# Sixteen transfers in place of twenty-four: joined tile loads and stores in a rotary-embedding kernel

## The chip, the cores and the metric

The kernel runs on one core of one Trainium2 chip. The metric is the device time of one execution in microseconds; the other cores are idle. The profile covers a span that is a little shorter than this time; the difference, 1.8 to 2.2 us, plays a part at the end of this study. DVE is the vector engine, POOL is GpSimd, PE the matrix engine, ACT the scalar engine; SP issues the transfers. PSUM is the small on-chip memory in which the kernel keeps its tables and products.

## The reference, cut to what matters

```python
batch, seq, dim = (16, 512, 1024)           # float32
num_heads = 16                              # head_dim 64, half_dim 32
x = x.reshape(batch, seq, num_heads, head_dim)
x1, x2 = x[..., :half_dim], x[..., half_dim:]
rotated = concatenate([x1 * cos - x2 * sin, x1 * sin + x2 * cos], axis=-1)
```

The input and the output are 33.55 MB each. Nothing is reused between batches, so each byte is moved once in and once out.

## The kernel before

Two batches make a tile of 128 partitions by 8 rows of 1024 numbers, 4 MiB; there are eight tiles and five buffers. DVE makes the cosine products and most sums, POOL most sine products, PE and ACT a part of the sums. Every transfer is issued by SP into one queue, which sixteen DMA engines work off. In the trace a tile is moved as 128 pieces of 32 KB, eight on each engine. A transfer has landed when its semaphore reports all of it; a seam is an engine's passage from one transfer to the next.

```python
def load(t, lo=0, hi=KK):
    if tiles[t] is None:
        tiles[t] = xp.tile([P, F], FP32, name="xt")          # pool of BUFS = 5
    s = slice(lo * dim, hi * dim)
    nc.sync.dma_start(out=tiles[t][:, s], in_=x_v[t][:, s])

load(0, 0, FIRST[0]) ... sin, cos ... rest of tile 0
for t in range(1, BUFS):
    load(t)
for i, n in enumerate(EXTRA):                                # four tiny loads
    nc.sync.dma_start(out=spare[:n, i], in_=sin_v[:n, :16])

tab = pfix.tile([P, BANK], FP32)                             # one PSUM tile for both tables
cos_t = tab[:, : KK * half]
sin_t = tab[:, KK * half : 2 * KK * half]

def stores(t):
    lo = 0
    for hi in LAST_OUT if t == NT - 1 else (KK,):            # LAST_OUT = (4, 8)
        store(t, lo, hi)
        lo = hi
    if t + 1 == NT - BUFS:                                   # after tile 2
        for n in range(BUFS, NT):
            load(n)                                          # tiles 5, 6, 7
# ... cut: the rotation itself, which the change does not touch
```

The tiny loads compute nothing. The transfers take eight semaphores in turn, and a transfer must wait for the one that had its semaphore eight places earlier. The tiny loads shift the count so that these waits fall where they do no harm.

## Time and profile before

| what | value | how to read it |
|---|---|---|
| time | 162.44 us | median of 3 runs, 162.35 to 162.64 |
| span of the profile | 160.7 us | first to last instruction of the program |
| DVE busy | 136.3 us, 85% | pauses only at the start and after its last tile |
| POOL busy | 127.1 us, 79% | second; waits for DVE to free its buffers |
| DMA queue | 98.0% of 16 engines' span | full from the second slice to the end |
| bytes | 67.25 MB | 33.69 read, 33.55 written |

The share of an engine that is busy does not by itself say what sets the end. Here two rows of the page are near full, DVE's and the DMA's.

### The profile page before, as it was taken

What the parts mean: (1) busy time and instruction counts of PE and PEld (TensorE: products, weight loads), DVE (VectorE), ACT (ScalarE), POOL (GpSimd) and SP (SyncE); (2) the same over time, 40 slices, a digit from 0 to 9 for tenths busy, and PEclk for the clock granted to TensorE, in tenths of its full rate; (3) what the DMA queues carried; (4) which work ended last, traced back from release to release, by engine and by line L of the source; (5) the groups of instructions that cost most, each with busy time, mean ns of one, the idle gap of its engine ahead of it and who ended that gap; (6) DMA issues with size and microseconds to landing.
All of it is one profiled execution on the core that took longest, in us unless ns stands there. A gap on an engine that the chain in (4) does not pass through costs nothing.

```text
span 160.7 us, 443 instructions
## 1 busy us (share of the span) xinstructions
PE 60.8 (38%) x71; PEld 19.3 (12%) x71; DVE 136.3 (85%) x85; ACT 18.7 (12%) x25; POOL 127.1 (79%) x38
## 2 busy tenths in 40 slices
PE   3041925056503931192308350664048402932000
PEld 0011301021102210131003010210022001300000
DVE  1059969999999999999999999999999999998000
ACT  0001311003000301012100310031003010211000
POOL 1039999999999999988998899898998899840000
PEclk9999995557655685559555855576556855595555
DMA  5999999999999999999999999999999999999994
GB/s 177 410 408 473 392 514 400 392 473 440 392 449 449 408 400 498 408 392 498 418 392 465 440 400 465 440 400 408 457 432 408 465 424 408 473 416 416 428 412 204
DMA packets 2787, 67.25 MB, mean 419 GB/s; under 512 B 354, under 2 KB 482, under 8 KB 482
## 3 DMA queue, kind: packets, MB, share of 16 engines
q1 hardware_dynamic: 2786, 67.24, 98.0%
q14 instruction: 1, 0.01, 0.0%
HBM read 33.69 MB, written 33.55 MB: 418 GB/s over the span
## 4 chain that ended last, share of the span: by engine, by line
DVE 68%; issue 12%; POOL 6%; DMA 4%; PE 1%; SPq 0%; DVEq 0%
DVE xt L189 33%; DVE pd L141 31%; POOL b L165 6%; DMA b<-in_sin_dram 4%; DVE pe_ps L141 3%; PE tab L113 1%; PE tab L114 1%; DVE sns L116 0%; DVE xt L150 0%; DVE own_ps L141 0%; SPq L74 0%; DVE sns L117 0%; DVEq L189 0%
## 5 line engine op out<-in xcount | busy, mean ns | idle before, releaser
L165 POOL TENSOR_TENSOR b<-xt,sns 128x2048 f32<-128x2048 f32 (+1 forms) x32 | 126.4, 3978 | 14.7 <-DVE sns L117 9.3
L189 DVE TENSOR_TENSOR xt<-pd,b 128x2048 f32<-128x2048 f32 x24 | 54.9, 2286 | 2.4 <-POOL b L165 1.6
L141 DVE TENSOR_TENSOR pd<-xt,tab 128x2048 f32<-128x2048 f32 x24 | 55.0, 2291 | 0.2
L176 PE MATMUL own_ps<-xt,ident 128*128 128x512 f32 x32 | 30.2, 1100 | 54.4 <-DVE xt L150 48.7
L176 PE MATMUL pe_ps<-b,ident 128*128 128x512 f32 x32 | 28.8, 1001 | 24.0 <-DVE pe_ps L141 24.0
L176 PEld LDWEIGHTS own_ps<-xt,ident 128*128 128x128 f32 x32 | 9.4, 323 | 74.3 <-DVE xt L150 59.7
L209 ACT COPY xt<-own_ps 128x1024 f32<-128x1024 f32 x8 | 8.1, 1012 | 73.7 <-PE own_ps L176 73.7
L181 ACT COPY xt<-pe_ps 128x512 f32<-128x512 f32 x16 | 9.4, 585 | 38.2 <-PE pe_ps L176 38.2
L176 PEld LDWEIGHTS pe_ps<-b,ident 128*128 128x128 f32 x32 | 8.4, 290 | 42.8 <-DVE pe_ps L141 34.1
L141 DVE TENSOR_TENSOR pe_ps<-xt,tab 128x512 f32<-128x512 f32 x16 | 11.0, 685 | 0.0
L141 DVE TENSOR_TENSOR own_ps<-xt,tab 128x1024 f32<-128x1024 f32 x8 | 9.8, 1223 | 0.0
L150 DVE TENSOR_TENSOR xt<-xt,tab 128x1024 f32<-128x1024 f32 x8 | 9.7, 1213 | 0.0
L116 DVE TENSOR_SCALAR sns<-tab 128x256 f32<-128x256 f32 x1 | 0.4, 424 | 8.2 <-PE tab L114 8.2
L113 PE MATMUL tab<-b,spread 64*128 64x256 f32 x2 | 1.2, 697 | 5.0 <-DMA b<-in_sin_dram 5.0
L209 ACT ACT_TABLE_LOAD x1 | 1.3, 1283 | 15.4 <-DVE xt L150 15.4
L101 PE MATMUL own_ps<-zero 128*128 128x512 bf16 x2 | 1.0, 618 | 1.2 <-DVE zero L97 1.2
L113 PEld LDWEIGHTS tab<-b,spread 64*128 64x128 f32 x2 | 0.5, 310 | 5.9 <-issue 5.9
L114 PE MATMUL tab<-b,spread 64*128 64x256 f32 x2 | 1.1, 631 | 0.0
L97 DVE MEMSET zero<- 128x256 uint32 x1 | 0.3, 272 | 0.9 <-PEq L240 0.9
L114 PEld LDWEIGHTS tab<-b,spread 64*128 64x128 f32 x2 | 0.7, 334 | 0.2
L101 PE MATMUL pe_ps<-zero 128*128 128x512 bf16 x1 | 0.6, 631 | 0.0
L101 PEld LDWEIGHTS <-zero 128*128 128x128 bf16 x3 | 0.3, 123 | 1.5 <-DVE zero L97 1.2
(9 smaller groups left out, 1.8 us busy)
## 6 DMA issues: line engine op xcount, KB each, us to landing
xt<-in_x_dram SPq DMA_DIRECT2D x7, 4096.0 KB, 29.8
out_dram<-xt SPq DMA_DIRECT2D x7, 4096.0 KB, 24.7
out_dram<-xt SPq DMA_DIRECT2D x2, 2048.0 KB, 10.2
xt<-in_x_dram SPq DMA_DIRECT2D x1, 2560.0 KB
xt<-in_x_dram SPq DMA_DIRECT2D x1, 1536.0 KB
b<-in_sin_dram SPq DMA_DIRECT2D x1, 64.0 KB
b<-in_cos_dram SPq DMA_DIRECT2D x1, 64.0 KB
spare<-in_sin_dram SPq DMA_DIRECT2D x1, 0.1 KB
```

What stands on the lines that cost most here:

```text
L97: nc.vector.memset(zero, 0.0)
L101: nc.tensor.matmul(out=ps, lhsT=zero[:, :P], rhs=zero, start=True, stop=True)
L113: nc.tensor.matmul(out=sin_t, lhsT=spread, rhs=sin_sb, start=True, stop=True)
L114: nc.tensor.matmul(out=cos_t, lhsT=spread, rhs=cos_sb, start=True, stop=True)
L116: nc.vector.tensor_scalar_mul(out=sns[:, :, 0, :], in0=sin_k, scalar1=-1.0)
L141: nc.vector.tensor_tensor(out=o, in0=i, in1=cb, op=ALU.mult)
L150: nc.vector.tensor_tensor(out=heads(r), in0=heads(r), in1=s, op=ALU.mult)
L165: nc.gpsimd.tensor_tensor(out=o, in0=i, in1=sb, op=ALU.mult)
L176: nc.tensor.matmul(out=ps, lhsT=ident, rhs=other, start=False, stop=True, skip_group_check=True)
L181: nc.scalar.copy(out=r, in_=pe_ps)
L189: nc.vector.tensor_tensor(out=r, in0=ps, in1=b, op=ALU.add)
L209: nc.scalar.copy(out=r0, in_=own_ps)
```

## The change

The intent is fewer, larger transfers: tiles 3 and 4 are loaded and stored together, tiles 6 and 7 loaded together, the tiny loads go, and the last tile is stored whole. That leaves sixteen transfers, two rounds of the eight semaphores. A second, separate change gives the sine table its own PSUM tile.

```diff
-BUFS = 5
+HOMES = (1, 2, 2)
-LAST_OUT = (4, 8)
-EXTRA = (2, 4, 5, 6)
+    def load_two(t):
+        nc.sync.dma_start(out=both(t), in_=x_v[t : t + 2].rearrange("t p f -> p t f"))
+    def store_two(t):
+        nc.sync.dma_start(out=out_v[t : t + 2].rearrange("t p f -> p t f"), in_=both(t))
-    for t in range(1, BUFS):
-        load(t)
-    ... the four tiny loads
+    load(1)
+    load(2)
+    load_two(3)
-    sin_t = tab[:, KK * half : 2 * KK * half]
+    sin_t = pd.tile([P, 2 * dim], FP32, name="pd")[:, : KK * half]
     def stores(t):
-        ... in LAST_OUT parts; loads 5, 6, 7 after tile 2
+        if t == 4:
+            store_two(3)
+        elif t != 3:
+            store(t)
+        if t == 2:
+            load(5)
+            load_two(6)
```

More of the change, by code (lines that the diff above doesn't have):

```diff
@@ L59 @@
     fixed = ctx.enter_context(tc.tile_pool(name="fixed", bufs=1))
-    xp = ctx.enter_context(tc.tile_pool(name="xp", bufs=BUFS))
+    xp = ctx.enter_context(tc.tile_pool(name="xp", bufs=1))
     bp = ctx.enter_context(tc.tile_pool(name="bp", bufs=3))
@@ L66, with both, store @@
     ctx.enter_context(tc.manual_schedule())
-    tiles = [None] * NT
+    homes = [xp.tile([P, n, F], FP32, name=f"x{n}{i}") for i, n in enumerate(HOMES)]
+    places = [home[:, i] for home, n in zip(homes, HOMES) for i in range(n)]
+    tiles = [places[t % len(places)] for t in range(NT)]
+    first_of = [sum(HOMES[:i]) for i in range(len(HOMES))]
+    def both(t):
+        return homes[first_of.index(t % len(places))]
     def load(t, lo=0, hi=KK):
-        if tiles[t] is None:
-            tiles[t] = xp.tile([P, F], FP32, name="xt")
         s = slice(lo * dim, hi * dim)
         nc.sync.dma_start(out=tiles[t][:, s], in_=x_v[t][:, s])
-    def store(t, lo=0, hi=KK):
-        s = slice(lo * dim, hi * dim)
-        nc.sync.dma_start(out=out_v[t][:, s], in_=tiles[t][:, s])
+    def load_two(t):
+        nc.sync.dma_start(out=both(t), in_=x_v[t : t + 2].rearrange("t p f -> p t f"))
+    def store(t):
+        nc.sync.dma_start(out=out_v[t], in_=tiles[t])
+    def store_two(t):
+        nc.sync.dma_start(out=out_v[t : t + 2].rearrange("t p f -> p t f"), in_=both(t))
     load(0, 0, FIRST[0])
@@ L87 @@
         load(0, lo, hi)
-    for t in range(1, BUFS):
-        load(t)
-    spare = fixed.tile([16, len(EXTRA), 16], FP32)
-    for i, n in enumerate(EXTRA):
-        nc.sync.dma_start(out=spare[:n, i], in_=sin_v[:n, :16])
+    load(1)
+    load(2)
+    load_two(3)
     ident = fixed.tile([P, P], FP32)
@@ L191, in stores @@
     def stores(t):
-        lo = 0
-        for hi in LAST_OUT if t == NT - 1 else (KK,):
-            store(t, lo, hi)
-            lo = hi
-        if t + 1 == NT - BUFS:
-            for n in range(BUFS, NT):
-                load(n)
+        if t == 4:
[5 more added lines that the diff above has]
+            load_two(6)
     cos_product(own_ps, rows(0, ROW_OWN), ROW_OWN)
```

## The prediction

> **What bounds the kernel now.** I read the page's busy tenths and queue first, then the chain that ended last, then the DMA queue's own waits, then single transfers by their issue time.
>
> The page, busy share of the 40 slices, the queue and the chain:
>
> ```profile
> DVE  1059969999999999999999999999999999998000
> ...
> DMA  5999999999999999999999999999999999999994
> ...
> q1 hardware_dynamic: 2786, 67.24, 98.0%
> ...
> DVE 68%; issue 12%; POOL 6%; DMA 4%; PE 1%; SPq 0%; DVEq 0%
> ```
>
> The chain is 68% DVE, which suggests a vector-bound kernel. But DVE is empty in the last three slices, while the DMA row stays at 9 from the second slice to the last but one and its one queue takes 98.0% of sixteen engines' span. The chain ends with the last vector instruction and does not count the queue behind it. So I ask how fast the queue drains. The answers for the issue lines, each cut to one transfer (load of tile 5, store of tile 5, second half of the last store): when it was issued, and how long until it landed.
>
> ```profile
> L74 SPq DMA_DIRECT2D xt<-in_x_dram x1: 793/793/793, 64.9 to 64.9; - x1
> ...
> DMA to landing us min/median/max: 26.9/26.9/26.9
> ```
>
> ```profile
> L78 SPq DMA_DIRECT2D out_dram<-xt x1: 333/333/333, 115.3 to 115.3; - x1
> ...
> DMA to landing us min/median/max: 25.2/25.2/25.2
> ```
>
> ```profile
> L78 SPq DMA_DIRECT2D out_dram<-xt x1: 332/332/332, 148.3 to 148.3; - x1
> ...
> DMA to landing us min/median/max: 11.6/11.6/11.6
> ```
>
> Load 5 lands at 64.9 + 26.9 = 91.8, store 5 at 115.3 + 25.2 = 140.5, the last half store at 148.3 + 11.6 = 159.9. Between the first two lie five transfers of 4 MiB (load 6, load 7, stores 3, 4, 5): 48.7 / 5 = 9.74 us each. From store 5 to the end lie two tiles: 19.4 / 2 = 9.70 us. The pitch is the same, 4.194 MB / 9.74 us = 431 GB/s, whether loads or stores are in line. A transfer waits some 15 us behind others, so the queue never empties. **The bound is bytes through one full queue**: the end is the start of the flow plus 16 tiles (loads and stores of 8) at 9.7 us. The vector engine is a close second. The windows around the end:
>
> ```profile
> 148.00:150.00 2.00, 0.00 (x0) 0.00 (x0) 0.24 (x1) 0.00 (x0) 0.00 (x0) 0.50 0.81 344
> 150.00:152.00 2.00, 0.00 (x0) 0.00 (x0) 0.00 (x0) 0.00 (x0) 0.00 (x0) 0.50 1.11 475
> ```
>
> (The third figure with a count is DVE; the last two are DMA share and GB/s.) DVE is done at 148.24; the queue runs on for ten microseconds. The trace's records of single DMA pieces, finer than these views, show it exactly: a 32 KB piece takes 1.21 us on its engine and the next begins within 0.02 us. The sixteen engines finish store 6 between 148.7 and 149.8, so they are up to 1.1 us apart, and the last piece of all ends at 159.5, on a late engine.
>
> **What the Trainium skill says.** "DMA: Bandwidth & Descriptors", Anatomy of one DMA, gives each DMA about 2 us of fixed cost, mostly the wait until the last byte is confirmed, but calls the semaphore write itself tiny, about one cycle. The trace agrees with the second: at a seam between transfers an engine shows a 4-byte piece of 0.01 us and goes on. So the 2 us shows only where the queue is empty. The same page, Where 436 GB/s comes from, sets 435.2 GB/s as the ports' ceiling; 431 here is 99% of it, so larger transfers have at most 1% to win. "SBUF — State Buffer", The DMA setup-cost knee, advises the largest transfers one can make; its reason is the fixed cost, which a full queue hides in this trace. The DMA page, Latency and other measured facts, has about 600 ns to the first byte; here the first transfer was issued at 0.73 and its first pieces start at 1.75, 1.0 us later.
>
> **The change, part by part.**
>
> 1. *Small loads removed.* Four transfers of 17 pieces of 64 bytes; each piece took 0.01 us in the piece records. Gain below 0.05 us. They were there to shift the eight rotating DMA semaphores. By the built order's waits, the sixteen transfers now fill these eight twice: every store and load waits only for what it needs (its own tile, or the store before it in that buffer), so no false wait appears.
>
> 2. *Two tiles in one transfer.* Three seams fewer at 0.02 us: 0.06 us. The pieces are the same 32 KB rows. What moves is when transfers are issued and when they count as landed. The queue's present waits:
>
> ```profile
> SPq L74 <- DMA out_dram<-xt: 15.9, 2, 9.6
> ```
>
> These are loads 6 and 7 waiting for stores 1 and 2 to land. The joint load waits for both, so it is issued at 82.2, as load 7 is now, ten microseconds later than load 6. The queue then still holds load 5 (landing 91.8, its flow ending about 90): no gap. Store 3 now waits for tile 4, 98.3 instead of 82.6, while load 6-7 lasts to 111.3: no gap. The order of bytes in the queue does not change.
>
> 3. *Tile 6 becomes visible late.* Both tiles land at 91.8 + 2 x 9.74 = 111.3 (slowest engine perhaps 111.5), where tile 6 alone landed at about 101.5. Who wants it, in the timeline of before:
>
> ```profile
> 109.17 11.30 POOL L165 TENSOR_TENSOR b<-xt,sns 128x2048 f32<-128x2048 f32 x3 [0.67 <-DVE xt L189]
> ...
> 111.80 1.22 DVE L141 TENSOR_TENSOR own_ps<-xt,tab 128x1024 f32<-128x1024 f32 x1
> ```
>
> POOL begins tile 6 at 109.17 and will wait over 2 us. It can afford it: products of 4.5, 2.35 and 4.5 us from 111.5 finish at 116.0, 118.4 and 122.9, and DVE uses the first at 118.6 and the third at 123.8. DVE's own first use at 111.80 is just after the landing. Joint load 3-4 lands at about 52.7, well before its use.
>
> 4. *Sine table in another PSUM tile.* The start of before:
>
> ```profile
> 8.67 1.06 PE L114 MATMUL tab<-b,spread 64*128 64x256 f32 x2
> 9.76 0.42 DVE L116 TENSOR_SCALAR sns<-tab 128x256 f32<-128x256 f32 x1 [8.21 <-PE tab L114]
> ```
>
> The copy waits for both products because they share a tile; now it needs only the sine, done at about 8.9. POOL and DVE start some 0.85 us earlier. Tiles then run 0.85 ahead until tile 6: DVE wants it at 110.95 and gets it at about 111.5, so it keeps only some 0.3 us. Its end goes from 148.24 to about 147.9. Off the bound either way.
>
> 5. *Last tile stored whole.* Now its first half is issued at 146.1 and keeps the queue fed. Whole, it is issued at about 148.0. With the 1.0 us to first pieces it can flow from 149.0. The early engines run out at 148.7 and idle 0.3 to 0.8 us; the late ones, at 149.8, do not notice, and they set the end. Eight pieces of 1.21 replace sixteen of 0.61: 9.68 instead of 9.76, minus 0.08 us.
>
> Sum: -0.05 - 0.06 - 0.08, about -0.2, plus perhaps 0.1 for restarting early engines. The span of 160.7 becomes about 160.5, the time **162.3 us** against 162.44.
>
> **Rivals.** *The split paid.* If the last store needs its full fixed cost after DVE's end, the end is 148.0 + 1.0 + up to 0.6 of stagger over the engines + 9.7 + 0.4 to land + 0.8 to close = 160.5; with a slow first piece (the first pieces of the run took up to 0.8 us longer than later ones) 161.3, a time near 163.0. For it: DMA share 0.81 in 148 to 150 already looks thin; against: late engines hide it. *Tile 6 holds the vector engine.* If POOL or DVE lost 2 us at tile 6 instead of nothing, the last store would be issued at 150.2 and the time would be near 164.5. For it: POOL's reserve is only about 0.6 us at the third product; against: the sums above. *Large transfers are faster.* If seams cost more than the records show, going from 24 transfers to 16 could win up to the distance to the ceiling, 1% or 1.6 us: near 160.8. Against: the two half stores take together 9.7 us, as one whole.
>
> **Range and chances.** The full queue pins the time; small gains and the late store pull opposite ways by some tenths. Range 161.8 to 163.3. Over 2% either way needs 3.2 us: more than the whole ceiling gap on the fast side, and a loss at tile 6 above the second rival's on the slow side. Faster 0.01, same 0.96, slower 0.03.
>
> **What would show it.** Right: DMA busy at 9 throughout; the joint load landing at 111 to 111.5 and POOL idle about 2 to 3 us just before; DVE starting 0.8 us sooner, ending near 147.9; last store about 148.0, landing near 159.9. Wrong: an idle slice in the queue (before 98.3 or at 148 to 150 on all engines), DVE waiting over 1 us on a product, or a pitch of other than 9.7 us in the joint transfers.

## The result, and the profile after

The changed kernel takes 162.79 us (median of 6 runs, 162.60 to 163.11) against 162.54 for the kernel before (6 runs, 162.27 to 162.85). The ratio is 1.0016 with a 95% interval of 1.0000 to 1.0032. A ratio is the mean time of one kernel's runs over that of the other's of the same rounds, so it is not quite the ratio of the two medians. 162.79 lies in the predicted range; but the forecast 162.3 had the sign of the small difference the other way round.

The page of the changed kernel, with the same rows as the prediction showed of before (busy tenths, queue, chain):

```profile
DVE  1079879999999999999999999998999999998000
...
DMA  5999999999999999999999999999999999999993
...
q1 hardware_dynamic: 2560, 67.24, 98.0%
...
DVE 43%; DMA 34%; issue 7%; POOL 7%; PE 1%; SPq 0%; DVEq 0%
```

The queue is as full as before, 98.0%, with 226 fewer pieces. The chain now gives DMA 34%, but the bound has not moved. The chain is followed back from the last vector instruction, and it now passes through DVE's short wait for tile 6, and from there through the queue. Before, it met no wait for a tile's load. A chain names one tight path of several.

The answers for the issue lines, joint load 6-7 and the last store (issue time in us, then the time to landing):

```profile
L80 SPq DMA_DIRECT2D x<-in_x_dram x1: 390/390/390, 82.3 to 82.3; - x1
DMA to landing us min/median/max: 29.1/29.1/29.1
```

```profile
L83 SPq DMA_DIRECT2D out_dram<-x x1: 333/333/333, 147.9 to 147.9; - x1
DMA to landing us min/median/max: 11.7/11.7/11.7
```

The joint load lands at 111.4, where load 7 was reckoned at 111.3 before. The last store lands at 159.6; its second half landed at 159.9 before. The start, and the arrival of tile 6, in the changed kernel's timeline (start, length, engine, work, idle time before it and who ended that):

```profile
8.87 0.42 DVE L122 TENSOR_SCALAR sns<-pd 128x256 f32<-128x256 f32 x1 [7.31 <-PE pd L119]
...
111.43 1.23 DVE L147 TENSOR_TENSOR own_ps<-x,tab 128x1024 f32<-128x1024 f32 x1 [0.43 <-DMA x<-in_x_dram]
111.47 31.54 POOL L171 TENSOR_TENSOR b<-x,sns 128x2048 f32<-128x2048 f32 x8 [3.65 <-DMA x<-in_x_dram]
```

DVE starts the sine copy at 8.87 instead of 9.76. It gives about half of that back at tile 6, where it waits 0.43 us; POOL waits 3.65 us there and then works without a pause. DVE's last instruction ends at 147.87, against 148.23 before. The windows around the end (last two figures: DMA share and GB/s):

```profile
148.00:150.00 2.00, 0.00 (x0) 0.00 (x0) 0.00 (x0) 0.00 (x0) 0.00 (x0) 0.50 0.81 344
150.00:152.00 2.00, 0.00 (x0) 0.00 (x0) 0.00 (x0) 0.00 (x0) 0.00 (x0) 0.50 1.07 459
```

The share in 148 to 150 is 0.81 as in the kernel before. In the trace's records of single pieces the engines end store 6 between 148.6 and 149.7, and the first pieces of the last store start at 148.78. At most 0.15 us is lost, and only on the early engines. In the second trace of the same kernel (`after_again`, below) the early engines lose up to 0.35 us. In both, the engine that ends last does not wait: it finishes store 6 at 149.66 (second trace 149.88), goes on within 0.01 us, and ends at 159.35 (159.56).

So nearly every step in the profile went as foreseen, and the span did what was forecast: 160.58 us in the mean of the six runs. In the next section's rounds the kernel before has 160.72 (11 runs). Yet the time rose. That is the question for the experiments, next to whether the bound is what I say.

### The profile page after: what moved, and what is told of

Same layout as the page of the kernel before. It is cut to its first block, busy times and chain, and to the rows that moved or that the text cites. A ratio compares the mean times of both kernels' runs of the same rounds, so it can differ in the third digit from the quotient of the medians.

```text
span 160.5 us, 429 instructions
## 1 busy us (share of the span) xinstructions
PE 60.8 (38%) x71; PEld 18.9 (12%) x71; DVE 136.3 (85%) x85; ACT 18.8 (12%) x25; POOL 126.9 (79%) x38
## 3 DMA queue, kind: packets, MB, share of 16 engines
q1 hardware_dynamic: 2560, 67.24, 98.0%
## 4 chain that ended last, share of the span: by engine, by line
DVE 43%; DMA 34%; issue 7%; POOL 7%; PE 1%; SPq 0%; DVEq 0%
DVE x L195 21%; DVE pd L147 18%; DMA x<-in_x_dram 18%; DMA out_dram<-x 12%; POOL b L171 7%; DMA b<-in_sin_dram 4%; DVE pe_ps L147 2%; PE pd L119 1%; DVE sns L122 0%; SPq L77 0%; DVE sns L123 0%; DVE own_ps L147 0%; DVE x L156 0%; DVEq L195 0%; SPq L80 0%
## 5 line engine op out<-in xcount | busy, mean ns | idle before, releaser
L171 POOL TENSOR_TENSOR b<-x,sns 128x2048 f32<-128x2048 f32 (+1 forms) x32 | 126.2, 3980 | 15.5 <-DVE sns L123 8.4
L195 DVE TENSOR_TENSOR x<-pd,b 128x2048 f32<-128x2048 f32 x24 | 54.9, 2286 | 2.3 <-POOL b L171 1.5
L147 DVE TENSOR_TENSOR pd<-x,tab 128x2048 f32<-128x2048 f32 x24 | 55.0, 2291 | 0.2
L182 PE MATMUL own_ps<-x,ident 128*128 128x512 f32 x32 | 30.2, 1099 | 54.9 <-DVE x L156 50.0
L182 PEld LDWEIGHTS own_ps<-x,ident 128*128 128x128 f32 x32 | 9.4, 324 | 74.5 <-DVE x L156 60.6
L215 ACT COPY x<-own_ps 128x1024 f32<-128x1024 f32 x8 | 8.1, 1012 | 75.0 <-PE own_ps L182 75.0
L187 ACT COPY x<-pe_ps 128x512 f32<-128x512 f32 x16 | 9.4, 586 | 37.6 <-PE pe_ps L182 37.6
L147 DVE TENSOR_TENSOR pe_ps<-x,tab 128x512 f32<-128x512 f32 x16 | 11.0, 686 | 0.0
L147 DVE TENSOR_TENSOR own_ps<-x,tab 128x1024 f32<-128x1024 f32 x8 | 9.8, 1224 | 0.5 <-DMA x<-in_x_dram 0.4
L156 DVE TENSOR_TENSOR x<-x,tab 128x1024 f32<-128x1024 f32 x8 | 9.7, 1213 | 0.0
```

Of the source, the lines that this page charges most:

```text
L147: nc.vector.tensor_tensor(out=o, in0=i, in1=cb, op=ALU.mult)
L156: nc.vector.tensor_tensor(out=heads(r), in0=heads(r), in1=s, op=ALU.mult)
L171: nc.gpsimd.tensor_tensor(out=o, in0=i, in1=sb, op=ALU.mult)
L182: nc.tensor.matmul(out=ps, lhsT=ident, rhs=other, start=False, stop=True, skip_group_check=True)
L187: nc.scalar.copy(out=r, in_=pe_ps)
L195: nc.vector.tensor_tensor(out=r, in0=ps, in1=b, op=ALU.add)
```

## The experiments

Twelve runs were made, each from the changed kernel with the edits shown (the first has none). "Kernel before" means its runs on the same chip in the same rounds. Spans and times are means or medians of runs as said.

### Is the 0.25 us real? The changed kernel again

No edit.

> The changed kernel once more, unedited, with more rounds, to see whether its 162.79 against 162.54 us is a real 0.2 us. Full-queue theory: span 160.4 to 160.9, ratio to the kernel before between 0.999 and 1.002. If the whole last store costs something real, the ratio is again about 1.0015 and its interval excludes 1.

Measured: 162.77 us (5 runs) against 162.50 (11 runs), ratio 1.0020, interval 1.0008 to 1.0032. The small loss is real. But the mean span is 160.62 against 160.72: inside the span the changed kernel is not slower. Time minus span is 2.22 us in the mean, against 1.79 for the kernel before. The loss lies outside the span; I return to it below.

### The last store in two halves again

```diff
-            store(t)
+            nc.sync.dma_start(out=out_v[t][:, :h], in_=tiles[t][:, :h])   # h = 4 * dim, last tile only
+            nc.sync.dma_start(out=out_v[t][:, h:], in_=tiles[t][:, h:])
```

> The change without its last part: the last tile is again stored in two halves, all else as changed. Full-queue theory: the DMA engines pass from store 6 to the last store without a pause in either version, so the time is that of the changed kernel within 0.3 us (162.4 to 162.9). Rival (the late whole store leaves the queue empty for about 1 us): 0.7 to 1.3 us faster than the changed kernel, near 161.8.

Measured: 162.77 us, the same as the unedited changed kernel; ratio to before 1.0016 (1.0003 to 1.0029). Storing the last tile whole cost nothing. The rival "the split paid" is refuted for this kernel's timing.

### Loads 6 and 7 apart again

```diff
-            load_two(6)
+            load(6)
+            load(7)
```

> The change with tiles 6 and 7 loaded by two transfers again. Tile 6 then lands near 101.6 us instead of 111.4, POOL's 3.65 us wait and DVE's 0.43 us wait for it vanish, and DVE ends near 147.4 instead of 147.87, the last store is issued that much earlier. Full-queue theory: the end stays, time within 0.3 us of the changed kernel. Rival (the vector engine's stall at tile 6 is on the path that sets the end): 0.4 us or more faster.

Measured: 162.54 us, ratio to before 1.0005 (0.9993 to 1.0018). In the wait view POOL's waits for loads are, in the changed kernel and then in this one (total, times, longest):

```profile
POOL b L171 <- DMA x<-in_x_dram: 5.1, 2, 3.7
```

```profile
POOL b L171 <- DMA x<-in_x_dram: 1.5, 1, 1.5
```

The wait for tile 6 is gone, DVE ends at 147.05 instead of 147.87 (147.4 was expected), and the last store is issued at 147.1. Its landing, 12.3 us later at 159.4, hardly moves. The mean span is 160.55 against 160.62. So 0.8 us of vector time bought less than 0.1 us in the span; the other 0.17 us of the gain are again outside it (2.05 instead of 2.22).

### The sine table back in its old place

```diff
-    sin_t = pd.tile([P, 2 * dim], FP32, name="pd")[:, : KK * half]
+    sin_t = tab[:, KK * half : 2 * KK * half]
```

> The change with the sine table back in the cosine's PSUM tile: DVE and POOL start about 0.87 us later (first sine copy at 9.7 instead of 8.87), then no wait for tile 6 is left on DVE, which ends near 148.2 instead of 147.87. The last store is issued near 148.2 and its first pieces start near 149.1, when the early DMA engines have been free for 0.4 us but the late ones have not. Full-queue theory: 0 to 0.4 us slower than the changed kernel. Rival (vector chain sets the end alone): 0.35 us slower at least, and 0.87 if the early start counts in full.

Measured: 163.18 us, 0.41 us slower than the unedited changed kernel; mean span 161.00 against 160.62. By its time alone this run cannot decide between the theories, since both allowed 0.4. A window shows the queue thin before the last store:

```profile
148.00:149.00 1.00, 0.00 (x0) 0.00 (x0) 0.29 (x1) 0.00 (x0) 0.00 (x0) 0.50 0.16 66
```

DVE now ends at 148.29 and the last store is issued at 148.4. The DMA share falls to 0.16 in that microsecond: by the piece records fifteen of the engines finish store 6 by 149.22 and wait up to 0.54 us for the last store. But this wait does not set the end. One engine alone still works on store 6 and ends last; in each of these two windows just one piece starts (41 GB/s over 0.8 us are 32 KB), and it is this engine's:

```profile
149.50:150.30 0.80, 0.00 (x0) 0.00 (x0) 0.00 (x0) 0.00 (x0) 0.00 (x0) 0.50 0.10 41
158.00:159.00 1.00, 0.00 (x0) 0.00 (x0) 0.00 (x0) 0.00 (x0) 0.00 (x0) 0.50 0.08 33
```

It finishes store 6 at 150.12, begins the last store at 150.13, and ends at 159.81; the others are done by 159.10. It was late already at the end of store 5, at 140.44 where the last engine of the changed kernel was at 139.98, eight microseconds before the last store was issued. So in this trace the loss is not the price of a late whole store. What delays the one engine is not shown, nor is it shown that this kernel needs the early sine table to afford a whole last store.

### A late last store, whole and in halves

```diff
         pair_sum(*p1, b1)
+        if t == NT - 1:
+            r = rows(t, third[0], 2)
+            nc.vector.tensor_tensor(out=r, in0=r, in1=r, op=ALU.max)
```

and, for the second run, the same with the last store in halves.

> One extra vector instruction of about 2.3 us on the last two rows (maximum of a value with itself, the result stays right) just before the last store, which is then issued near 150.2 instead of 147.9. In the changed kernel the last store's first pieces start 0.02 to 0.12 us after the engines' last pieces of store 6, so there is hardly any reserve left: expected 1.4 to 2.2 us slower than the changed kernel (the late engines hide up to 1 us). If there were still reserve in the queue: no change.

> The same extra 2.3 us instruction, with the last tile stored in two halves. The first half is issued near 145.7 and keeps the engines busy to about 153.6; the second is issued near 150.2, well before that. Full-queue theory: no change against the changed kernel (within 0.3 us), 1.4 to 2.2 us faster than the late whole store. So the half store that the change removed would be a reserve of some 3 us against a late vector end, which the kernel before did not need.

Measured: whole 164.81 us, 2.0 us slower than the changed kernel (162.79), mean span 162.53. In halves 162.78 us, mean span 160.57, no change. The windows of the late whole store:

```profile
149.00:150.00 1.00, 0.00 (x0) 0.00 (x0) 1.00 (x1) 0.00 (x0) 0.00 (x0) 0.50 0.00 0
150.00:151.00 1.00, 0.00 (x0) 0.00 (x0) 0.29 (x1) 0.00 (x0) 0.00 (x0) 0.50 0.00 0
151.00:152.00 1.00, 0.00 (x0) 0.00 (x0) 0.00 (x0) 0.00 (x0) 0.00 (x0) 0.50 1.22 524
```

No piece starts for over two microseconds, first while DVE works and then until the store's first pieces start at 151.19. Now even the late engine, done with store 6 at 149.79, must wait. So the changed kernel has little reserve left there: 2.3 us of extra vector work become 2.0 us of time. The half store is a reserve of at least those 2.3 us, which the changed kernel without the extra work did not need.

### Which wall is the bound? Less vector work, fewer bytes, both

Three kernels: the first leaves out the third pair of rows; the second does not store tile 0; the third does both. Their outputs are wrong, which doesn't matter for the times.

```diff
-        b1 = sin_rows(t, third[0], 2)
-        p1 = pair_product(t, third[0])
-        pair_sum(*p1, b1)                  # less vector work: the last pair of each tile
```

```diff
-        elif t != 3:
+        elif t not in (0, 3):              # fewer bytes: tile 0 is never stored
             store(t)
```

> Wrong result on purpose: rows 6 and 7 of each tile are stored as loaded, so DVE loses two 2.29 us instructions per tile (36 us of busy time in all) and POOL one of 4.5 us. Full-queue theory: the same 67.24 MB pass the queue at the same pace, DVE ends some 12 us earlier and the time stays within 0.5 us of the changed kernel. Rival (vector-bound, as the chain of the page before says): tens of microseconds faster, about 125 to 130 us.

> Wrong result on purpose: tile 0 is computed but never stored, so the queue carries 4.19 MB less, worth 9.7 us at its pace. If the queue alone set the end, the time would fall by 9.7 us to about 153. My theory is that the vector chain is a second wall at nearly the same place: DVE still ends near 147.4 (no wait for tile 6 any more), the last store is issued then, takes 0.9 us to its first pieces and 9.7 us to flow, so the time falls by only 0.5 to 1.5 us, to about 161.5.

> Wrong result on purpose: both cuts at once, rows 6 and 7 unrotated and tile 0 not stored. With both walls moved the whole 9.7 us of the missing store should appear: about 153 us (152 to 154). If either cut alone already gives this, the theory of two walls at one place is wrong.

| kernel | time us | mean span us | DVE busy us | queue MB |
|---|---|---|---|---|
| changed (six runs) | 162.79 | 160.58 | 136.3 | 67.24 |
| less vector work | 162.86 | 161.03 | 100.8 | 67.24 |
| fewer bytes | 161.56 | 159.43 | 136.3 | 63.05 |
| both | 153.07 | 151.32 | 100.8 | 63.05 |

A quarter of DVE's work removed alone wins nothing. The rows of that page:

```profile
DVE  1079879969995995999700199632995999400000
...
DMA  5999999999999999999999999999999999999993
```

DVE has holes everywhere; the DMA row is what it was. (Its span is even 0.4 us longer. Again one engine ends last without a pause: it finishes store 6 at 150.11 and the last store at 159.79, though that store was issued at 141.3. What delays it is open.) A sixteenth of the bytes removed alone wins only 1.2 us, not 9.7. Two windows of that kernel:

```profile
62.00:64.00 2.00, 0.00 (x0) 0.00 (x0) 1.97 (x2) 0.00 (x0) 2.00 (x1) 0.50 0.00 0
...
146.00:148.00 2.00, 0.00 (x0) 0.00 (x0) 1.31 (x1) 0.00 (x0) 0.00 (x0) 0.50 0.00 0
```

The queue now stands empty while DVE and POOL work, and the last store (issued at 147.4, landing 11.1 us later) waits for DVE. Only both cuts together give the missing store's 9.7 us: 162.79 - 153.07 = 9.72. (0.4 us of this lies outside the span. From the kernel with less vector work to the one with both cuts, the span alone falls by 161.03 - 151.32 = 9.71.) There are two walls, the queue and the vector chain plus one store, and they stand within about a microsecond of each other.

### What does a seam between transfers cost?

Every transfer of 4 or 8 MiB is cut into transfers of 2 MiB: 30 transfers in place of 16.

```diff
+        cuts = (0, 4, 8) if (lo, hi) == (0, KK) else (lo, hi)
+        for a, b in zip(cuts, cuts[1:]):
+            s = slice(a * dim, b * dim)
             nc.sync.dma_start(out=tiles[t][:, s], in_=x_v[t][:, s])   # stores likewise, joint ones apart
```

> Every 4 or 8 MiB transfer of the changed kernel cut into transfers of 2 MiB (30 in all, 16 KB pieces). Theory that a seam costs 0.02 us in a full queue: 14 more seams, 0 to 0.5 us slower. Rival (each transfer costs part of its fixed 2 us, so merging pays): 14 more transfers, several microseconds slower, and merging three pairs would have been worth 0.5 us or more.

Measured: 163.53 us, 0.74 us slower than the changed kernel, ratio to before 1.0057 (1.0015 to 1.0100). This is above the 0 to 0.5 that I expected, and far below the several microseconds of the rival. The last store, issued at 147.0, lands 13.2 us later at 160.2, 0.6 us after the changed kernel's 159.6. That is 0.04 us for each of the 14 more transfers, pieces of half the size included; against the second trace of the changed kernel, which landed at 159.9, it is 0.02, and the 0.74 us of time give 0.05. A further part of the span arises after the queue: SP's wait for the last barrier, in the changed kernel and then here:

```profile
SPq L260 <- PEq L260: 0.6, 2, 0.4
```

```profile
SPq L266 <- PEq L266: 0.9, 2, 0.8
```

The longest such wait is 0.4 us longer with no transfer left, which is why the span grew more than the landing. It is no loss of time: time minus span fell by about as much, from 2.22 to 1.87.

### The loss outside the span

```diff
     make_identity(nc, ident)
+    pad = fixed.tile([P, 24], FP32)
+    for i in range(24):
+        nc.gpsimd.memset(pad[:, i : i + 1], 0.0)
```

> The changed kernel with 24 one-column memsets on POOL while it waits for the sine table (transfers and results unchanged). In the runs so far the time minus the profiled span is a fixed number per kernel: 1.8 us for the kernel before, 2.2 for the changed one, 2.05 with loads 6 and 7 apart, 1.8 for the cuts with fewer POOL instructions and for the halves. It goes with the number of POOL records in the trace (60 gives 2.2, 61 gives 2.05; 55, 62 and 69 give 1.8), so I suspect that the changed kernel's 0.25 us lies outside the span and comes from where POOL's program ends, not from transfers. If so: span 160.4 to 160.9 as before, difference 1.8, time near 162.4, 0.4 us faster than the changed kernel. If the transfers cause it: difference stays 2.2, time near 162.8.

Measured: 162.42 us against 162.60 for the kernel before, ratio 0.9987 (0.9970 to 1.0004). Time minus span is 1.80 in the mean, down from 2.22; the mean span is 160.65, unchanged. Twenty-four instructions that do nothing useful made the program 0.4 us shorter outside the span. The same transfers with a padded POOL program lose nothing, so the loss is not a cost of moving the bytes. (The unpadded kernel was not run on this chip. On the three others the kernels with its POOL program have 2.20 to 2.22; the kernel before has 1.79 to 1.80 on all four.) What in the program decides is not shown. Its length alone does not order the runs: with less vector work POOL has fewer instructions than the changed kernel, cut into halves it has more, and both have about 1.8 (1.83 and 1.87). One line of the page changes along, for the changed kernel and then for the padded one:

```profile
q14 instruction: 1, 0.01, 0.0%
```

```profile
q14 instruction: 2, 0.02, 0.0%
```

By the piece records the second one is 8 KB of instructions at 115.9. It would fit a fetch that the padding moves from the end of the program into its run, but no record here shows such a fetch at the end of the changed kernel, so the mechanism stays open.

### The best of both

Loads 6 and 7 apart, the last store in halves, the padding, and the rest of the change.

```diff
-            load_two(6)
+            load(6)
+            load(7)
```

(and the last store in halves and the padding, as above)

> The best of both by the experiments: the early sine table and joint load 3-4 and store 3-4 of the change, loads 6 and 7 apart (no wait for tile 6), the last tile stored in two halves, and the POOL padding. The queue is still full from start to end, so it can win only tenths: span 160.2 to 160.7, time 162.0 to 162.5, against 162.5 for the kernel before. More than 0.5 us faster than before would contradict the full-queue theory.

Measured: 162.52 us against 162.60, ratio 0.9995 (0.9977 to 1.0012). It is not distinguishable from the kernel before. No version found here beats it, which is what two full walls allow.

## Why the prediction was right or wrong

**The bound: right.** The prediction called the queue the bound and DVE a close second. The three cuts show both, and how close the second is.

**Small loads and seams (steps 1 and 2): right.** Removing eight transfers changed the queue's pace by nothing that the runs resolve: the last landing moved by 0.3 us in the profiles, the mean span by 0.1 us. The wait order was as read from the program: the joint load was issued at 82.3 (82.2 forecast). The joint store went at 97.4; I had written 98.3, today's end of tile 4, and forgot to take the early start off.

**Tile 6 (step 3): right, with a wait undersized.** The landing at 111.4 was within the forecast 111.3 to 111.5. POOL waited 3.65 us, not 2 to 3, because it comes to tile 6 sooner, at 107.8 instead of 109.2, mostly by the early start. DVE's wait was 0.43 us and the products came in time, so the rival "tile 6 holds the vector engine" failed: putting loads 6 and 7 apart moved the span by less than 0.1 us.

**Sine table (step 4): right in size, its conclusion open.** Start 8.87 (8.9 forecast), DVE's end 147.87 (147.9). "Off the bound either way" does not fit the 0.4 us by which the mean span of five runs is longer without it; but the one trace puts this on a DMA engine that was late before the last store, and why it was is not shown.

**Last tile whole (step 5): right, for the reason given, by a narrow margin.** First pieces came 0.8 us after issue (1.0 reckoned). The early engines paused, by up to 0.15 us in one trace and 0.35 in the other (0.3 to 0.8 reckoned); the late one, which sets the end, did not, and it did not with the old table place either. With the store issued 2.4 us later it had to wait as well. (One reading under the rival was slightly off: the slowest of the run's first pieces took 1.0 us longer than later ones, not 0.8.)

**The sum: the term that was missing.** The forecast -0.2 us held for the span, which fell by about 0.1. The step that failed was the last one, from span to time, where I let a span 0.2 us shorter stand for a time 0.2 us shorter. Time minus span rose by 0.43 us, from 1.79 to 2.22, and the padding run took it back; no term of the prediction's sum stood for it. The net +0.3 in these rounds is -0.1 and +0.4.

**The rival of larger transfers** failed as foreseen: 14 more transfers cost 0.7 us of time in all, so three joins could win no more than about 0.15 us by that measure.

## What to carry to other kernels

When a queue is full from start to end, joining transfers of this size wins almost nothing; ask instead which bytes can go, and check that the engine behind the queue is not a second wall at the same place. The last store is the one transfer whose fixed cost is bare: keep it small or early unless the engines are still busy when it is issued. A window's mean over sixteen engines can show a gap that costs nothing, because the engine that is furthest behind sets the end: look for its pieces. Compare spans as well as times when a difference is below half a percent, since a few tenths of a microsecond can come from outside the profile.

## What the Trainium skill lacked or had wrong

- "DMA: Bandwidth & Descriptors", Anatomy of one DMA and Rules for kernel authors: about 2 us fixed per DMA, and advice to join small ones. The page does not give the cost of one more transfer in a full queue. Here an engine went on within 0.02 us at a seam by the piece records, and 14 more transfers cost 0.02 to 0.05 us each. Bare, the last 4 MiB store took 11.1 us, near an estimate from the page's fit, 2.0 + 9.6 = 11.6 us, although that fit is for the other descriptor path (transfers issued by GpSimd).
- "DMA: Bandwidth & Descriptors", Latency and other measured facts: about 600 ns to the first byte; the page does not say from where it counts. From the start of the issuing instruction to the first piece it was 1.0 us at the start of the run and 0.8 us at the last store; from that instruction's end 0.6 and 0.5 us.
- "SBUF — State Buffer", The DMA setup-cost knee: larger single transfers are advised as such. Joining two of 4 MiB moved the span by about 0.1 us at most, and delayed the first tile's landing by 10.0 us (101.4 to 111.4).
- I found no page that has this: the time outside the profiled span depends on a kernel's own instructions. It was 1.8 us before, 2.22 after the change, and 1.8 again with 24 idle POOL instructions.
